# Operand work of the up units moved later in the MLP of a two-layer decoder trunk, and split in two parts

## The chip, the cores and the metric

The kernel runs on one core of one Trainium2 chip. The metric is device time in microseconds (us) of one execution; lower is better. The kernel before takes 2268.28 us, the median of 3 runs (2266.05 to 2270.3).

The engines of the core work side by side, each through its own queue in order: TensorE (PE; its weight loads are listed as PEld), VectorE (DVE), ScalarE (ACT), GpSimd (POOL), and SyncE (SP), which issues the DMA transfers. Matrix products add up in PSUM, which has eight banks of 128 x 512 f32.

## The reference

Two layers work on x of 256 tokens by 2048 features, all in float32. The attention part of each layer (a gated linear attention and a stick-breaking attention side by side, and an output projection added to x) is untouched by the change but for its last addition. What matters here is the second half of a layer:

```python
hm = rms_norm(x, mlp_norm)
up = jnp.square(jax.nn.relu(jnp.einsum('bsd,df->bsf', hm, w_up)))     # 2048 -> 8192
return x + jnp.einsum('bsf,fd->bsd', up, w_down)                       # 8192 -> 2048
```

## The kernel before

**Products.** Each f32 matrix is split into a high part (rounded by an ACT copy to the matmul's fp32r form) and a low part (a DVE subtraction: the value less its high part). A product of two blocks is three matmuls: high x high, high x low weights, low x high weights (`mm`, lines 989 to 998). So for each block of weights that the DMA brings (tile `raw`), ACT makes `whi` (L985) and DVE makes `wlo` (L986), with four tiles of each.

**Units and steps.** The MLP of a layer is 16 units: for each quarter q of the 8192 hidden features up 0, up 1, down 0, down 1. A unit is 8 steps, j = 0 to 7; each multiplies a 256 x 256 piece of the operand by 256 x 1024 weights. Steps 1, 3 and 5 are "fast": they use seven block products in place of eight, for which DVE first forms sums of weight blocks (`ts` at L1118, then two additions through `add`, L1001), and which need further sums of the operand's blocks (`sx`). A fast step is four products with 6, 3, 6 and 6 matmuls, any other step is two with 12 each, so a unit is 22 products, k = 0 to 21, and 183 matmuls. Step j=1 is k = 2 to 5, j=3 is k = 8 to 11, j=5 is k = 14 to 17.

**Order.** In the MLP the order of PE, DVE and ACT is written out by hand. The main loop (L1188 to 1207) prepares the weights of product k+3 (ACT and DVE rows) and then emits product k on PE (`emit`, L1173), so weights are prepared four products ahead. After emitting product k it runs what hangs on k: the tail of the unit (k = 17: sums of four banks; 20 and 21: the other four) and the entries of the table that `begin` returns (L1149). So a row that hangs on k stands in the queues of ACT and DVE behind the preparation of product k+3 and ahead of that of k+4.

**Operands.** The result of an up unit has to become the operand of the down units. In the unit that follows (the second up unit, or the first down unit), `begin` gives: at k = 0 and 1 `turn`: PE transposes the result into banks 5, 7 and 1, 6, eight transposes each, and ACT squares them into `t` (L1086); at k = 3, 4, 9, 10 `operand`, which calls `forms` for the four pieces. `forms` makes high and low part of a piece through `split` (L294: an ACT copy, L295, and a DVE subtraction, L296). For a fast piece (number 1, 3 or 5 of the eight) it first does four DVE subtractions (L305 to 308) into `e`, splits `e` into `sx` and then the piece itself. The second up unit makes pieces 0 to 3, of which 1 and 3 are fast; the first down unit makes 4 to 7, of which 5 is fast, and uses them itself, from j=4 (k = 12) on.

**Start of the MLP.** The output projection adds into `acc` tiles of two banks; `residual` (L940) adds the result to x. For the last of the four blocks of columns, `residual(3, uo)` stands in the MLP's loop, behind the preparation of product 2. The MLP's banks take the place of the projection's `acc` and `ps` tiles in PSUM, in the order in which they are first asked for: 2, 4, 5, 7, 3, 8, 1, 6, so banks 2 and 4 of the first product lie on the last projection's `acc`. The last block of x is turned and becomes an operand after product 0 (`norm_operand`, L339 on DVE, banks 5 and 7).

## Time and profile before

| | |
|---|---|
| median of 3 runs | 2268.28 us (2266.05 to 2270.3) |
| profiled execution | 2270.26 us, of which the span from the first to the last instruction is 2268.6 |
| busy, share of the span | PE 2213.3 us (98%), DVE 1825.4 (80%), ACT 1250.8 (55%), POOL 38.0 (2%) |
| mean granted TensorE clock | 0.989 |
| DMA | 408.96 MB, mean 180 GB/s |
| MLP of the first layer | 419.88 us to some 1135 us of the span; of the second from 1546.27 us to the end |

In the profile, "busy" is the time in which an engine's instructions run. A row of a timeline gives start and duration in us, engine, source line, operation, the tile written and the tiles read, and in brackets the idle time before it and what ended that. "x3" means that three like rows in a row are merged. In a window's row each engine has its busy time and, in brackets, its instructions; then come the granted clock, the DMA's share and GB/s. The granted clock is a share of TensorE's full rate.

### The profile page before, as it was taken

To read this page: it belongs to the slowest core of one execution; us is meant where nothing else is said; L and a number is where in the kernel's file an instruction comes from. 1 tells how busy PE (TensorE), PEld (TensorE's weight loads), DVE (VectorE), ACT (ScalarE), POOL (GpSimd) and SP (SyncE) were. 2 spreads that over 40 slices of the span, in tenths; PEclk is the share of its full clock that TensorE was granted. 3 is DMA by queue.
4 is the path that set the end of the run, shared out by engine and by line. 5 is a ranking of instruction groups with operands and counts; after the bars stand their busy time and mean duration, and the time that the engine had idled before them with its cause. 6 is when DMAs were issued, how large, how long until landed. Compare 5 with 4: busy or idle time off the path is not lost.

```text
span 2268.6 us, 27081 instructions
## 1 busy us (share of the span) xinstructions
PE 2213.3 (98%) x10376; PEld 1822.8 (80%) x10376; DVE 1825.4 (80%) x2286; ACT 1250.8 (55%) x1623; POOL 38.0 (2%) x64
## 2 busy tenths in 40 slices
PE   9999999999999999999999999999999999999999
PEld 7988778777877877877888887887778778778777
DVE  5777566789988989988966765667899889889888
ACT  5555355555565556455556553555655555654664
POOL 0020000000000000000000200000000000000000
PEclk9999999999999999999999999999999999999999
DMA  6554446454545555555446543555455545455544
GB/s 226 186 165 153 149 148 240 165 190 164 215 171 174 213 184 177 202 186 185 152 157 195 171 162 133 185 204 188 165 186 199 185 173 202 171 186 212 187 158 146
DMA packets 152549, 408.96 MB, mean 180 GB/s; under 512 B 6650, under 2 KB 31810, under 8 KB 152420
## 3 DMA queue, kind: packets, MB, share of 16 engines
q1 hardware_dynamic: 152420, 407.24, 51.8%
q8 instruction: 81, 1.33, 0.2%
q14 instruction: 48, 0.39, 0.1%
HBM read 405.12 MB, written 2.10 MB: 180 GB/s over the span
## 4 chain that ended last, share of the span: by engine, by line
PE 85%; DVE 11%; ACT 3%; issue 1%; DMA 0%; SPq 0%; POOL 0%; ACTq 0%
PE acc L412 9%; PE acc L413 9%; PE acc L414 9%; DVE wlo L986 4%; PE acc L459 3%; PE acc L463 1%; DVE act L296 1%; DVE ts L1118 1%; ACT whi L985 1%; DVE raw L1001 1%; DVE t L1001 1%; ACT act L1086 1%; DVE sx L296 1%; ACT sx L295 1%; PE ps L882 1%
## 5 line engine op out<-in xcount | busy, mean ns | idle before, releaser
L986 DVE TENSOR_TENSOR wlo<-raw,whi 128x1024 fp32r<-128x1024 f32 x512 | 610.1, 1221 | 82.4 <-ACT whi L985 79.3
L985 ACT ACTIVATE whi<-raw 128x1024 fp32r<-128x1024 f32 x512 | 532.8, 1056 | 198.4 <-PE acc L414 10.0
L395 DVE TENSOR_TENSOR wlo<-raw,whi 128x1024 fp32r<-128x1024 f32 (+2 forms) x274 | 317.5, 1165 | 194.9 <-ACT whi L393 193.7
L393 ACT ACTIVATE whi<-raw 128x1024 fp32r<-128x1024 f32 (+2 forms) x274 | 273.5, 1004 | 290.9 <-PE acc L414 243.1
L412 PE MATMUL acc<-whi,act 128*128 128x512 f32 (+2 forms) x960 | 368.7, 384 | 1.6 <-ACT act L337 1.6
L413 PE MATMUL acc<-wlo,act 128*128 128x512 f32 (+2 forms) x960 | 362.4, 378 | 0.0
L414 PE MATMUL acc<-whi,act 128*128 128x512 f32 (+2 forms) x960 | 362.0, 377 | 0.0
L985 ACT ACTIVATE whi<-t 128x512 fp32r<-128x512 f32 x96 | 60.7, 632 | 280.6 <-DVE t L1001 189.1
L412 PEld LDWEIGHTS acc<-whi,act 128*128 128x128 f32 x960 | 181.1, 189 | 36.8 <-issue 4.1
L414 PEld LDWEIGHTS acc<-whi,act 128*128 128x128 f32 x960 | 180.8, 188 | 34.0 <-issue 0.7
L413 PEld LDWEIGHTS acc<-wlo,act 128*128 128x128 f32 x960 | 181.1, 189 | 31.7 <-DVE wlo L395 0.8
L986 DVE TENSOR_TENSOR wlo<-ts,whi 128x1024 fp32r<-128x1024 f32 x96 | 117.6, 1225 | 16.3 <-ACT whi L985 16.3
L1118 DVE TENSOR_TENSOR ts<-raw 128x1024 f32<-128x1024 f32 x96 | 117.0, 1219 | 0.0
L985 ACT ACTIVATE whi<-ts 128x1024 fp32r<-128x1024 f32 x96 | 100.5, 1047 | 0.0
L459 PE MATMUL acc<-act,whi 128*128 128x512 f32 x256 | 91.9, 402 | 0.0
L463 PE MATMUL acc<-act,wlo 128*128 128x256 f32 x256 | 71.8, 280 | 0.0
L1047 ACT ACTIVATE act<-act,st 128x512 f32<-128x512 f32 x64 | 44.6, 720 | 48.7 <-DVE act L1001 48.7
L1001 DVE TENSOR_TENSOR raw<-ts,raw 128x512 f32<-128x512 f32 x96 | 66.4, 692 | 3.3
L1001 DVE TENSOR_TENSOR t<-raw 128x512 f32<-128x512 f32 x96 | 66.4, 692 | 3.3
L986 DVE TENSOR_TENSOR wlo<-t,whi 128x512 fp32r<-128x512 f32 x96 | 65.7, 684 | 0.0
L459 PEld LDWEIGHTS acc<-act,whi 128*128 128x128 f32 x256 | 48.1, 188 | 11.1
L295 ACT ACTIVATE sx<-t 128x384 fp32r<-128x384 f32 x24 | 12.6, 526 | 69.6 <-DVE t L308 69.6
(2384 smaller groups left out, 4670.7 us busy)
## 6 DMA issues: line engine op xcount, KB each, us to landing
raw<-in_w_up_dram SPq DMA_DIRECT2D x128, 1024.0 KB, 5.1
raw<-in_w_down_dram SPq DMA_DIRECT2D x128, 1024.0 KB, 5.4
raw<-in_w_in_dram SPq DMA_DIRECT2D x84, 1024.0 KB, 5.1
raw<-in_w_o_dram SPq DMA_DIRECT2D x32, 1024.0 KB, 5.0
raw<-in_w_in_dram SPq DMA_DIRECT2D x14, 512.0 KB, 6.7
raw<-in_w_in_dram SPq DMA_DIRECT2D x8, 544.0 KB, 3.7
out_dram<-xb SPq DMA_DIRECT2D x8, 256.0 KB, 2.0
xb<-in_x_dram SPq DMA_DIRECT2D x3, 512.0 KB, 8.0
```

The source lines that it names most:

```text
L296: nc.vector.tensor_tensor(d[:, :, 1, :], t, f32(d[:, :, 0, :]), ALU.subtract)
L393: newest["hi"] = nc.scalar.activation(h, r, AF.Copy).ins
L395: newest["lo"] = nc.vector.tensor_tensor(lo[:, q : q + step, :width], r, f32(h), ALU.subtract).ins
L412: nc.tensor.matmul(o, xh[:, sl], whi[:, j, :width], start=first, stop=False)
L413: nc.tensor.matmul(o, xh[:, sl], wlo[:, j, :width], start=False, stop=False)
L414: st["mm"] = nc.tensor.matmul(o, xl[:, sl], whi[:, j, :width], start=False, stop=last).ins
L459: nc.tensor.matmul(acc[:, f, :], whi[:, j, sl], op.both(k), start=(k == 0), stop=False, skip_group_check=True,)
L463: nc.tensor.matmul(acc[:, f, T:], wlo[:, j, sl], xh, start=False, stop=(k == KT - 1), skip_group_check=True,)
L985: nc.scalar.activation(hi[:, :n], r, AF.Copy)
L986: nc.vector.tensor_tensor(lo[:, :n], r, f32(hi[:, :n]), ALU.subtract)
L1001: nc.vector.tensor_tensor(dst, a, b, ALU.subtract if sub else ALU.add)
L1118: nc.vector.tensor_tensor(t13, ends, b12.unsqueeze(1).to_broadcast([P, 2, 512]), ALU.add)
```

## The change

Four edits, all in the MLP:

1. `split` does its ACT copy at once and returns the DVE subtraction as a function; `forms` returns a function that does the subtractions of its pieces. `begin` runs that function one product later than `forms`.
2. The squares leave `turn` and become `square`, one product later: at k = 1 and 2.
3. The pieces are made at k = 4, 10, 13 and 15 (before 3, 4, 9, 10), their low parts at 5, 11, 14 and 16.
4. The MLP's banks are asked for at once, in the order 5, 7, 1, 6, 2, 4, 3, 8; and `residual(3, uo)` stands behind the preparation of product 1, no longer of product 2.

```diff
+    def new_bank(m):
+        return pools["m"].tile([P, 512], F32, tag=f"m{m}", name=nm(f"m{m}_"))
+    unused = {}
     def mlp_psum():
         open_scope("psum", m=1)
+        unused.update((m, new_bank(m)) for m in (5, 7, 1, 6, 2, 4, 3, 8))
     def bank(m):
-        return pools["m"].tile([P, 512], F32, tag=f"m{m}", name=nm(f"m{m}_"))
+        return unused.pop(m, None) or new_bank(m)
...
     def split(d, t):
         nc.scalar.activation(d[:, :, 0, :], t, AF.Copy)
-        nc.vector.tensor_tensor(d[:, :, 1, :], t, f32(d[:, :, 0, :]), ALU.subtract)
+        return lambda: nc.vector.tensor_tensor(
+            d[:, :, 1, :], t, f32(d[:, :, 0, :]), ALU.subtract
+        )
     def forms(op, i, t, tag):
+        lows = []
...
-            split(d, e)
-        split(op.pair(i), t)
+            lows.append(split(d, e))
+        lows.append(split(op.pair(i), t))
+        return lambda: [low() for low in lows]
...
-                nc.scalar.activation(t[:, i].rearrange("p j t -> p (j t)"), pt, AF.Square)
+        def square(u, h):
+            y = ys[u]
+            t = y["t", h] = act_tile(F32, (P, 2, 2, T))
+            for i in range(2):
+                nc.scalar.activation(
+                    t[:, i].rearrange("p j t -> p (j t)"), y["p", h, i], AF.Square
+                )
         def operand(u, i):
...
-            forms(op, 4 * n2 + i, ys[u]["t", i // 2][:, i % 2], "sx")
+            ys[u]["low", i] = forms(op, 4 * n2 + i, ys[u]["t", i // 2][:, i % 2], "sx")
...
-            return {
-                0: lambda: turn(p, 0), 1: lambda: turn(p, 1),
-                3: lambda: operand(p, 0), 4: lambda: operand(p, 1),
-                9: lambda: operand(p, 2), 10: lambda: operand(p, 3),
+            work = {
+                0: lambda: turn(p, 0),
+                1: lambda: (turn(p, 1), square(p, 0)),
+                2: lambda: square(p, 1),
             }
+            for i, k in enumerate((4, 10, 13, 15)):
+                work[k] = lambda i=i: operand(p, i)
+                work[k + 1] = lambda i=i: ys[p]["low", i]()
+            return work
...
-                    if x == 1 and i == 0:
+                    if x == 0 and i == 1:
                         residual(3, uo)
```

What moves, at three places. In the rows, `wlo` and `whi` are the low and high parts of weights, `raw` the weights as loaded, `ts` and `t` the sums of a fast step (and `t` also the sums `e` of a fast piece), `act` the pieces and their sources, `sx` the rounded sums of a fast piece. The lines of the changed kernel are numbered 8 to 19 higher (L986 is L999 there, L296 is L304, L1118 is L1137, L1001 is L1014, L985 is L998, L295 is L303).

The first place is DVE in the first layer's unit 1 (a second up unit), from the low part of product 7 to that of product 8. Before:

```order
L986 TENSOR_TENSOR wlo_4076<-raw_728_3871,whi_4075 128x1024
L305 TENSOR_TENSOR t_775_4087<-act_4009 128x128
L306 TENSOR_TENSOR act_4009<-act_4009 128x128
L307 TENSOR_TENSOR t_775_4087<-act_4009 128x128
L308 TENSOR_TENSOR t_775_4087<-act_4009,t_775_4087 128x128
L296 TENSOR_TENSOR sx_4088<-t_775_4087,sx_4088 128x3x128
L296 TENSOR_TENSOR act_4095<-act_4009,act_4095 128x2x256
L1118 TENSOR_TENSOR ts_4100<-raw_733_3890 128x1024
L1001 TENSOR_TENSOR raw_733_3890<-ts_4100,raw_733_3890 128x512
L1001 TENSOR_TENSOR t_780_4101<-raw_733_3890 128x512
L986 TENSOR_TENSOR wlo_4106<-raw_733_3890,whi_4105 128x1024
```

Now:

```order
L999 TENSOR_TENSOR wlo_4073<-raw_728_3871,whi_4072 128x1024
L1137 TENSOR_TENSOR ts_4088<-raw_733_3890 128x1024
L1014 TENSOR_TENSOR raw_733_3890<-ts_4088,raw_733_3890 128x512
L1014 TENSOR_TENSOR t_777_4089<-raw_733_3890 128x512
L999 TENSOR_TENSOR wlo_4094<-raw_733_3890,whi_4093 128x1024
L304 TENSOR_TENSOR act_4084<-act_4047,act_4084 128x2x256
L999 TENSOR_TENSOR wlo_4107<-t_777_4089,whi_4106 128x512
```

The four subtractions and two low parts of fast piece 1 have left this place; the low part of piece 0, which stood ahead of product 7's part, follows product 8's. Piece 1's subtractions now stand at the same place one fast step later, ahead of the `ts` of product 14, and its two low parts behind product 14's.

The second place is ACT in the same unit, from the high part of product 17 on. Before (L1055 copies a bank for the unit's tail):

```order
L985 ACTIVATE whi_4241<-raw_3964 128x1024
L985 ACTIVATE whi_4253<-raw_4063 128x1024
L985 ACTIVATE whi_4260<-raw_4063 128x1024
L985 ACTIVATE whi_4272<-raw_778_4098 128x1024
L1055 ACTIVATE act_4282<-m__783_4109 128x512
```

Now:

```order
L998 ACTIVATE whi_4229<-raw_3964 128x1024
L998 ACTIVATE whi_4242<-raw_4063 128x1024
L303 ACTIVATE sx_4250<-t_811_4249 128x3x128
L303 ACTIVATE act_4256<-act_4060 128x2x256
L998 ACTIVATE whi_4258<-raw_4063 128x1024
L998 ACTIVATE whi_4272<-raw_775_4086 128x1024
L1068 ACTIVATE act_4282<-m__780_4097 128x512
```

The two high parts of fast piece 3 now stand ahead of product 19's. On DVE, at the same place of the changed kernel:

```order
L304 TENSOR_TENSOR act_4227<-act_4060,act_4227 128x2x256
L999 TENSOR_TENSOR wlo_4243<-raw_4063,whi_4242 128x1024
L317 TENSOR_TENSOR t_811_4249<-act_4060 128x128
L318 TENSOR_TENSOR act_4060<-act_4060 128x128
L319 TENSOR_TENSOR t_811_4249<-act_4060 128x128
L320 TENSOR_TENSOR t_811_4249<-act_4060,t_811_4249 128x128
L999 TENSOR_TENSOR wlo_4259<-raw_4063,whi_4258 128x1024
L304 TENSOR_TENSOR sx_4250<-t_811_4249,sx_4250 128x3x128
L304 TENSOR_TENSOR act_4256<-act_4060,act_4256 128x2x256
L999 TENSOR_TENSOR wlo_4273<-raw_775_4086,whi_4272 128x1024
```

Piece 3's subtractions follow product 18's low part, and product 19's low part follows them with no sums of a fast step between. In a first down unit the piece made here (7) isn't fast, and only its one low part stands behind product 19's.

The third place is DVE at the start of the first layer's MLP, from product 1's low part to that of product 3. Before (`xb_104` is the last block of x):

```order
L986 TENSOR_TENSOR wlo_3613<-raw_656_3598,whi_3612 128x1024
L1118 TENSOR_TENSOR ts_3618<-raw_657_3600 128x1024
L1001 TENSOR_TENSOR raw_657_3600<-ts_3618,raw_657_3600 128x512
L1001 TENSOR_TENSOR t_667_3619<-raw_657_3600 128x512
L986 TENSOR_TENSOR wlo_3624<-raw_657_3600,whi_3623 128x1024
L940 TENSOR_TENSOR xb_104<-acc_3420,xb_104 128x1024
L986 TENSOR_TENSOR wlo_3629<-t_667_3619,whi_3628 128x512
```

Now:

```order
L999 TENSOR_TENSOR wlo_3621<-raw_664_3606,whi_3620 128x1024
L953 TENSOR_TENSOR xb_104<-acc_3420,xb_104 128x1024
L1137 TENSOR_TENSOR ts_3627<-raw_665_3608 128x1024
L1014 TENSOR_TENSOR raw_665_3608<-ts_3627,raw_665_3608 128x512
L1014 TENSOR_TENSOR t_675_3628<-raw_665_3608 128x512
L999 TENSOR_TENSOR wlo_3633<-raw_665_3608,whi_3632 128x1024
L999 TENSOR_TENSOR wlo_3637<-t_675_3628,whi_3636 128x512
```

The last addition to x has moved ahead of the sums of step 1. The first product's banks, 2 and 4, now lie on the projection's `ps` tiles, and banks 5, 7, 1 and 6 on its two `acc` tiles. On PE, SP and POOL the order of instructions is the same in both kernels.

More of the change, by code (lines that the diff above doesn't have):

```diff
@@ L329, in norm_operand @@
                     )
-                forms(op, 2 * n + h2, t, "sxh")
+                forms(op, 2 * n + h2, t, "sxh")()
                 continue
@@ L1075, in turn @@
             y = ys[u]
-            t = y["t", h] = act_tile(F32, (P, 2, 2, T))
             for i in range(2):
-                pt = bank(((5, 7), (1, 6))[h][i])
+                pt = y["p", h, i] = bank(((5, 7), (1, 6))[h][i])
                 for j in range(2):
```

## The prediction

> **What bounds the kernel now.** I read the page first, then the unit lengths in windows, then what TensorE (PE) waits for, then the granted clock around one wait, then the chain of waits that leads into it.

> ```profile
> PE 2213.3 (98%) x10376; PEld 1822.8 (80%) x10376; DVE 1825.4 (80%) x2286; ACT 1250.8 (55%) x1623; POOL 38.0 (2%) x64
> ```

> PE is busy 98% of the span of 2268.6 us, so only its gaps and its clock can give time. Units are the 16 blocks of 8 steps of a layer's MLP, numbered 0 to 15 in the order up 0, up 1, down 0, down 1. Windows over five units (columns: length, then busy time of PE, weight loads, VectorE (DVE), ScalarE (ACT), GpSimd, then clock):

> ```profile
> 462.70:511.00 48.30, 45.48 (x200) 36.97 (x200) 42.41 (x53) 28.94 (x38) 0.00 (x0) 0.96 0.50 173
> 511.00:558.30 47.30, 45.21 (x200) 37.10 (x200) 42.28 (x51) 27.87 (x35) 0.00 (x0) 0.96 0.46 159
> 558.30:599.80 41.50, 41.50 (x184) 34.34 (x184) 39.05 (x44) 21.75 (x23) 0.00 (x0) 1.00 0.57 204
> 599.80:641.30 41.50, 41.50 (x184) 34.38 (x184) 37.67 (x41) 22.40 (x25) 0.00 (x0) 1.00 0.62 224
> 869.70:915.40 45.70, 43.63 (x201) 35.77 (x199) 41.92 (x51) 27.67 (x35) 0.00 (x0) 1.00 0.47 164
> ```

> Units 3 and 4 (rows three and four) have no operand work and run at PE's pace: 183 matmuls in 41.5 us, 0.227 us each. Units 1, 2 and 10 (the first two rows and the last) turn the up unit before them and make its operands; they take 45.7 to 48.3 us, and 16 of the 32 units are of this kind. Their 16 transposes cost some 2 us (unit 10: 45.7, less 41.5, less one gap of 2.2), so such a unit at PE's pace would take 43.5 us. DVE is busy 42.4 us in unit 1: it has about 1 us to spare in those 43.5.

> What PE waits for (the source line of the second matmul of a product, whose weights are the low part that DVE makes):

> ```profile
>   DVE wlo L986: 43.0, 24
> ```

> 24 gaps hold 43.0 us of idle; counted from matmul start to matmul start, less the normal 0.23, about 47 us. One of them in PE's timeline:

> ```profile
> 710.82 0.50 PE L997 MATMUL m__1134_5775<-wlo,act 128*128 128x512 f32 x1 [2.07 <-DVE wlo L986]
> ```

> Windows of PE alone (length, busy, clock), and the mean clock:

> ```profile
> 708.50:711.90 3.40, 1.33 (x7) 1.00 0.00 1
> 711.90:715.30 3.40, 3.40 (x10) 0.51 0.15 22
> 886.00:889.40 3.40, 1.51 (x7) 1.00 0.34 137
> 889.40:892.80 3.40, 3.21 (x14) 1.00 0.00 0
> ```
> ```profile
> core 0: 2268.6 us, clock 0.989
> ```

> They show a second price: after the gap of 2.07 us, which leaves PE busy 1.33 of 3.4 us, the next 3.4 us run at clock 0.51; where the busy part was 1.51 (a gap across two windows) the clock stays 1.00. The mean clock of 0.989 is 0.011 x 2268.6 = 25 us lost, some 14 such windows at 1.7 us. Gaps and slow clock together: about 71 us. The chain of waits into the gap at 673.8 us (unit 5):

> ```profile
> 655.39 0.30 DVE t L308
> 655.71 0.54 ACT sx L295
> 656.27 0.56 DVE sx L296
> 656.83 0.65 DVE act L296
> 657.49 1.15 DVE ts L1118
> ...
> 660.08 2.71 DVE wlo L986 x3
> ```

> The four subtractions of a fast operand end, ACT rounds the result, DVE waits and makes two low parts, and only then starts on the sums of the next fast step. All of it stands between two low parts that PE needs.

> **The change, part by part.** No row moves on PE, SP or POOL, and no step that moves issues a DMA; what moves is on DVE and ACT. Product k below is the k-th of a unit's 22; each low part is queued some four products ahead. How far ahead, in a unit without operand work, the clean unit 4 shows:

> ```profile
> 620.43 1.22 DVE L1118 TENSOR_TENSOR ts<-raw 128x1024 f32<-128x1024 f32 x1
> ...
> 623.02 1.22 DVE L986 TENSOR_TENSOR wlo<-raw,whi 128x1024 fp32r<-128x1024 f32 x1
> 624.15 0.69 DVE L986 TENSOR_TENSOR wlo<-t,whi 128x512 fp32r<-128x512 f32 x1
> 624.84 1.23 DVE L986 TENSOR_TENSOR wlo<-ts,whi 128x1024 fp32r<-128x1024 f32 x1
> 627.05 4.80 DVE L986 TENSOR_TENSOR wlo<-raw,whi 128x1024 fp32r<-128x1024 f32 x4 [0.99 <-ACT whi L985]
> ...
> 634.42 2.35 DVE L986 TENSOR_TENSOR wlo<-raw,whi 128x1024 fp32r<-128x1024 f32 x2
> ```

> On PE, the matmul of that unit's product 14 that reads the low part; and on DVE, unit 3's low part of product 21 (the first of the three):

> ```profile
> 625.93 0.39 PE L997 MATMUL m__982_5069<-wlo,act 128*128 128x512 f32 x1
> ```
> ```profile
> 595.45 3.49 DVE L986 TENSOR_TENSOR wlo<-raw,whi 128x1024 fp32r<-128x1024 f32 x3
> ```

> Product 14's low part ends at 624.24 and PE needs it at 625.93: spare 1.7 us. Counting 0.227 us per matmul onward, the spare is 2.4 at product 15, 1.85 at 16, 1.0 at 17, 1.15 at 18, 2.7 at 19, 4.3 at 20 and 3.2 at 21 (row 634.42); in the down unit before it 21 has only 0.7 (row 595.45), since eight additions precede it. DVE idles once, 0.99 us before product 17's part.

> *Gap at product 8 (step j=3).* Gone from ahead of it: four subtractions, ACT's turn, two low parts and operand 0's, some 3.7 us. Operand 0's low part now follows product 8's, and 0.6 us fits the spare of the later ones. The squares leave ACT's queue for one and two prepared parts later; the banks they free are first needed at products 4 and 5, and PE takes 2.7 us for each of products 0 and 1, which covers them. I take this gap, and its half clock, as gone: spare about 1.5 us.

> *Product 14 to 18 (j=5, j=6).* Inserted now: subtractions 1.3 (four at 0.33 pitch) ahead of 14, low parts of 0.5 and 0.6 ahead of 15. Spare 1.7 - 1.3 = 0.4 at 14; 2.4 - 2.4 = 0 at 15; 1.85 - 2.4 = -0.6 at 16. A stall of about 0.7 with the 0.1 that lies between a part's end and its matmul when PE waits. In the down unit the same operand is used at once: its low part ends 1.1 us after product 14's, so PE waits 0.6 there, inside the same 0.7. The idle 0.99 before 17 absorbs part; operand 2's low part adds 0.6: 2.4 - 1.0 + 0.6 = 2.05 against 1.15 at 18. Lost so far: 0.95.

> *Product 19 in a second up unit.* Operand 3 is fast there: four subtractions on DVE, and in ACT's queue its two high parts now stand ahead of product 19's high part, with nothing on DVE between. The same sequence in unit 1 of before, on DVE and on ACT:

> ```profile
> 476.77 0.29 DVE L308 TENSOR_TENSOR t<-act,t 128x128 f32<-128x128 f32 x1
> ```
> ```profile
> 477.09 0.53 ACT L295 ACTIVATE sx<-t 128x384 fp32r<-128x384 f32 x1 [2.94 <-DVE t L308]
> 477.52 0.62 ACT L295 ACTIVATE act<-act 128x512 fp32r<-128x512 f32 x1
> 478.05 1.04 ACT L985 ACTIVATE whi<-raw 128x1024 fp32r<-128x1024 f32 x1
> ```

> From the last subtraction's start to the end of the following high part: 2.3 us, where DVE would need 0.33 to go on. Before, the sums of a fast step lay behind it and filled DVE's time; now DVE waits 2.05. Charge at 19: 2.05 + 1.3 + 2.05 = 5.4 against 2.7. Lost so far 2.8, of which the new gap is some 1.5 us of idle in two pieces. At 20 and 21 two more low parts (1.1): 6.5 against 3.2. Lost in the whole unit: about 3.4 us.

> *Product 21 in a first down unit.* Operand 7 isn't fast, so no turn of ACT; its low part adds 0.6: 2.05 + 0.6 = 2.65 against 0.7. Lost: 2.1 us, and the next unit, which starts with DVE 0.6 later than before, loses about 0.2.

> *Start of the MLP.* PE's wait for the last residual block goes, but not what hangs on it:

> ```profile
> 419.88 0.47 PE L995 MATMUL m__672_3632<-whi,act 128*128 128x512 f32 x1 [1.92 <-DVE xb L940]
> ```
> ```profile
> 418.52 1.22 DVE L940 TENSOR_TENSOR xb<-acc,xb 128x1024 f32<-128x1024 f32 x1
> ...
> 423.86 0.49 DVE L339 SCALAR_TENSOR_TENSOR act<-m__674_3646,gcol_b,act 128x256 fp32r<-128x256 f32 x1 [3.52 <-ACT act L337]
> ...
> 427.25 1.23 DVE L986 TENSOR_TENSOR wlo<-ts,whi 128x1024 fp32r<-128x1024 f32 x1 [0.47 <-ACT whi L985]
> ```

> The accumulator is complete at about 418.0, and the addition now starts near 418.1. The sums of step 1 (2.6 us) and two low parts (1.8) used to run largely before that and now follow: 418.1 + 1.15 + 2.6 + 1.8 = 423.65 for the first L339, 0.2 earlier than 423.86. From there to product 4's low part nothing changes (3.4 us). PE starts 2.1 us earlier and waits about 1.9 more at product 4. I count 0.2 per layer, 0.4 in all; the ends are 0 and the whole 4.2.

> **The sum.** 8 x (3.4 + 2.1 + 0.2) = 45.6 us come back of the 71; with 0.4 from the start the gain is 26 us. No half-clock window is left in it: the largest new gap leaves PE busy about 1.9 of 3.4 us, above the 1.51 that kept the clock. The profiled execution took 2270.26 us (1.7 outside the span), 2 above the median of 2268.28; I take the gain off the median: 2242 us.

> [...]

> **The rivals.**
> - *ACT's turn is covered.* If product 19's high part waited for nothing, units lose 1.35 (1.95 fewer, at 19 to 21), 2.1 and 0.2: 29 us return, 2226 us. For it: ACT is busy only 29 of 48 us. Against: its queue is in order, and rows 477.09 to 478.05 show the high part starting right behind.
> - *The half clock comes at the new gap.* If 1.5 us of idle are enough, 8 windows at 1.7 us: 2256 us. Against: the row with 1.51 busy, idle 1.9, at full clock after.
> - *Slower.* The same mechanism, grown: the gap at product 19 and the one at product 21 of the down unit each last 0.8 us longer, PE falls under 1.45 busy in a 3.4 us window, and both cost a half window. Per group 5.7 + 2 x (0.8 + 1.7) = 10.7, in all 86 against 71: 2283 us. For it: DVE has 1 us to spare per unit. It decides where a gap leaves PE less than 1.45 busy.
> [...]

> **How the numbers follow.** Forecast 0.62, covered turn 0.15, half clock 0.12, slower 0.05, windows stay 0.03, elsewhere 0.03. The range 2225 to 2257 reaches to the second and third case. A measurement of this kernel tells about 0.2% (4.5 us) from no change; faster by more: 0.62 + 0.15 + 0.12 + 0.01 = 0.90, within 0.05, slower 0.05.

> **What would show it.** Right: no PE wait at product 8; second up units near 46.9 us, first down units near 45.6, clock 1.00 in them; a PE wait on the low part at product 19, behind ACT's high part, behind the fast operand's rounding; the first product of the MLP at once, and a wait at its fifth. Wrong: units 1 and 2 at 43.5 (DVE had more room than counted), or clock 0.5 windows still there.

## The result and the profile after

The changed kernel takes 2238.25 us, the median of 4 runs (2237.89 to 2238.47), beside 2268.76 us for the kernel before (4 runs, 2266.05 to 2270.3). The ratio is 0.9867, with a 95% interval of 0.985 to 0.9884: 30.5 us less. The profiled executions differ by 32.4 us: 2237.89 against 2270.26, and spans of 2236.2 against 2268.6; that of before lies 1.5 us above the median, that of the changed kernel 0.4 below. The line numbers of the new kernel are those given with the change (`whi` L998, `wlo` L999, the three matmuls of a product L1008, L1010, L1011, additions L1014).

The page's first part, and the clock:

```profile
PE 2201.8 (98%) x10376; PEld 1800.9 (81%) x10376; DVE 1818.7 (81%) x2286; ACT 1246.2 (56%) x1623; POOL 38.0 (2%) x64
```
```profile
core 0: 2236.2 us, clock 1.000
```

PE's share looks as before, and says little: a matmul at half clock counts as busy (PE is busy 3.41 of 3.41 us at clock 0.50 in a row of the squares alone, below). The clock says more. It was 0.989 and is 1.000, so no window at half clock is left in the MLP. The windows over the same five units (1, 2, 3, 4 and 10; length, then PE, weight loads, DVE, ACT, GpSimd, clock):

```profile
462.10:508.60 46.50, 44.79 (x200) 35.48 (x199) 40.94 (x52) 27.17 (x36) 0.00 (x0) 1.00 0.46 158
508.60:554.00 45.40, 44.25 (x200) 35.76 (x200) 42.86 (x53) 29.18 (x37) 0.00 (x0) 1.00 0.53 187
554.00:595.60 41.60, 41.60 (x184) 34.42 (x185) 39.17 (x44) 21.67 (x23) 0.00 (x0) 1.00 0.57 206
595.60:637.00 41.40, 41.40 (x184) 34.31 (x183) 37.58 (x41) 22.37 (x25) 0.00 (x0) 1.00 0.61 224
858.60:903.90 45.30, 44.17 (x199) 35.65 (x200) 42.75 (x53) 29.11 (x37) 0.00 (x0) 1.00 0.53 186
```

Unit 1 went from 48.3 to 46.5 us and unit 2 from 47.3 to 45.4. Counted from first matmul to first matmul, the eight second up units took 390.4 us together and now take 372.1, the eight first down units 376.7 and now 362.8: 32.2 us less in 16 units. Before, their lengths varied (48.2 to 49.6, depending on where the half clock fell); now all second up units lie between 46.50 and 46.53. Units 3 and 4 are as they were. The spans differ by 32.4, so the gain lies in the units whose operand work moved.

What PE waits for, by the releaser of the second matmul of a product (low part of the weights), and of the first:

```profile
  DVE wlo L999: 15.2, 26
```
```profile
  ACT whi L998: 4.3, 10
  DVE act L1014: 1.4, 8
  DVE xb L1014: 0.9, 5
```

The low parts cost 15.2 us of idle instead of 43.0. No wait is left at product 8. DVE there (unit 1) runs from the sums of the fast step straight to product 8's low part, and piece 0's follows it:

```profile
474.29 1.22 DVE L1137 TENSOR_TENSOR ts<-raw 128x1024 f32<-128x1024 f32 x1
...
476.88 1.22 DVE L999 TENSOR_TENSOR wlo<-raw,whi 128x1024 fp32r<-128x1024 f32 x1
478.01 0.68 DVE L304 TENSOR_TENSOR act<-act,act 128x512 fp32r<-128x512 f32 x1
```

The new waits stand at the end of the unit. PE in unit 1: product 19 twice, product 21, and the next unit's first product:

```profile
498.42 0.50 PE L1008 MATMUL m__759_4023<-whi,act 128*128 128x512 f32 x1 [0.42 <-ACT whi L998]
499.68 0.50 PE L1010 MATMUL m__759_4023<-wlo,act 128*128 128x512 f32 x1 [0.76 <-DVE wlo L999]
...
505.66 0.50 PE L1010 MATMUL m__759_4023<-wlo,act 128*128 128x512 f32 x1 [0.25 <-DVE wlo L999]
...
508.63 0.47 PE L1008 MATMUL m__836_4375<-whi,act 128*128 128x512 f32 x1 [0.18 <-DVE act L1014]
```

DVE and then ACT at the same place:

```profile
496.05 0.29 DVE L320 TENSOR_TENSOR t<-act,t 128x128 f32<-128x128 f32 x1
498.40 1.22 DVE L999 TENSOR_TENSOR wlo<-raw,whi 128x1024 fp32r<-128x1024 f32 x1 [2.06 <-ACT whi L998]
```
```profile
496.38 0.53 ACT L303 ACTIVATE sx<-t 128x384 fp32r<-128x384 f32 x1 [3.92 <-DVE t L320]
496.81 0.62 ACT L303 ACTIVATE act<-act 128x512 fp32r<-128x512 f32 x1
497.33 1.99 ACT L998 ACTIVATE whi<-raw 128x1024 fp32r<-128x1024 f32 x2
```

This is the chain of the prediction: the fourth subtraction ends, ACT (idle 3.92 us until then) rounds both parts of the piece, only then product 19's weights, and DVE idles 2.06 us.

The start of the MLP, on PE (first product and product 4) and on DVE:

```profile
417.54 0.39 PE L1008 MATMUL m__659_3599<-whi,act 128*128 128x512 f32 x1
...
426.61 0.50 PE L1008 MATMUL m__691_3709<-whi,act 128*128 128x512 f32 x1 [0.52 <-ACT whi L998]
427.87 0.50 PE L1010 MATMUL m__691_3709<-wlo,act 128*128 128x512 f32 x1 [0.76 <-DVE wlo L999]
```
```profile
417.74 1.23 DVE L953 TENSOR_TENSOR xb<-acc,xb 128x1024 f32<-128x1024 f32 x1 [3.12 <-PE acc L427]
418.88 1.22 DVE L1137 TENSOR_TENSOR ts<-raw 128x1024 f32<-128x1024 f32 x1
```

PE starts 2.3 us earlier and gives most of it back at product 4: unit 0 ends at 462.12 instead of 462.74. Of these 0.6 us, 0.26 lie ahead of the MLP: the projection's last matmul ends at 417.70 in this profile and at 417.96 in that of before. DVE idles 3.12 us for the accumulator with the sums of step 1 queued behind the addition.

### The profile page after: what moved, and what is told of

The parts are those of the page before. It is cut to its first block, busy times and chain, and to the rows that moved or that the text cites. A ratio compares the mean times of both kernels' runs of the same rounds, so it can differ in the third digit from the quotient of the medians.

```text
span 2236.2 us, 27047 instructions
## 1 busy us (share of the span) xinstructions
PE 2201.8 (98%) x10376; PEld 1800.9 (81%) x10376; DVE 1818.7 (81%) x2286; ACT 1246.2 (56%) x1623; POOL 38.0 (2%) x64
## 3 DMA queue, kind: packets, MB, share of 16 engines
q8 instruction: 81, 1.33, 0.2%
## 4 chain that ended last, share of the span: by engine, by line
PE 81%; DVE 15%; issue 2%; ACT 1%; DMA 0%; SPq 0%; POOL 0%; DVEq 0%; ACTq 0%
PE acc L425 9%; PE acc L426 9%; PE acc L427 9%; DVE wlo L999 7%; PE acc L472 3%; PE acc L476 1%; DVE xb L1014 1%; ACT whi L998 1%; DVE t L1014 1%; DVE act L304 1%; DVE ts L1137 1%; DVE act L1014 1%; DVE sx L304 1%; PE ps L895 1%; PE ps L907 1%
## 5 line engine op out<-in xcount | busy, mean ns | idle before, releaser
L999 DVE TENSOR_TENSOR wlo<-raw,whi 128x1024 fp32r<-128x1024 f32 x512 | 610.4, 1220 | 96.4 <-ACT whi L998 92.9
L998 ACT ACTIVATE whi<-raw 128x1024 fp32r<-128x1024 f32 x512 | 528.8, 1054 | 185.2 <-PE acc L427 10.0
L998 ACT ACTIVATE whi<-t 128x512 fp32r<-128x512 f32 x96 | 60.8, 633 | 268.7 <-DVE t L1014 143.0
L999 DVE TENSOR_TENSOR wlo<-ts,whi 128x1024 fp32r<-128x1024 f32 x96 | 117.4, 1223 | 1.4 <-ACT whi L998 1.4
L1137 DVE TENSOR_TENSOR ts<-raw 128x1024 f32<-128x1024 f32 x96 | 116.7, 1216 | 0.0
L998 ACT ACTIVATE whi<-ts 128x1024 fp32r<-128x1024 f32 x96 | 100.4, 1046 | 0.0
L1014 DVE TENSOR_TENSOR raw<-ts,raw 128x512 f32<-128x512 f32 x96 | 66.4, 692 | 3.3
L1014 DVE TENSOR_TENSOR t<-raw 128x512 f32<-128x512 f32 x96 | 66.4, 692 | 3.3
L999 DVE TENSOR_TENSOR wlo<-t,whi 128x512 fp32r<-128x512 f32 x96 | 65.7, 684 | 0.0
L303 ACT ACTIVATE sx<-t 128x384 fp32r<-128x384 f32 x24 | 12.6, 526 | 73.9 <-DVE t L320 73.9
```

The lines of the kernel that those rows point to most:

```text
L998: nc.scalar.activation(hi[:, :n], r, AF.Copy)
L999: nc.vector.tensor_tensor(lo[:, :n], r, f32(hi[:, :n]), ALU.subtract)
L1014: nc.vector.tensor_tensor(dst, a, b, ALU.subtract if sub else ALU.add)
L1137: nc.vector.tensor_tensor(t13, ends, b12.unsqueeze(1).to_broadcast([P, 2, 512]), ALU.add)
```

## The experiments

The theory was the prediction's: the chain subtractions, rounding, low parts ahead of a product's low part is what stopped PE; splitting it takes the wait away, moving it puts its remains at product 19; and the half clock follows the long gaps. Twelve kernels tested its steps. Beside them the kernel before had medians of 2266.5 to 2268.5 us; each ratio is against the runs of the same chip.

### Each edit alone, on the kernel before

**Edit 4 alone** (banks and last residual block):

```diff
-        return pools["m"].tile([P, 512], F32, tag=f"m{m}", name=nm(f"m{m}_"))
+        return unused.pop(m, None) or new_bank(m)
...
-                    if x == 1 and i == 0:
+                    if x == 0 and i == 1:
                         residual(3, uo)
```

> Kernel before with the fourth edit alone (order of the banks, last residual block behind product 1). Theory (the wait is only moved: the addition now stands ahead of the sums of step 1, so product 4 waits instead): the 1.92 us wait at each layer's first product is gone, a wait of about 1.3 us in two pieces stands at product 4, and the time falls by 0.5 to 1 us, to about 2268. Rival (the wait at the start is a loss of its own): 4.2 us less, 2264.5, and no wait at product 4.

Measured: 2266.85 us, ratio 0.9989 (0.9976 to 1.0002), no difference that can be told; the rival's 4.2 us lie in this interval too, so the time does not decide. The waits do: the one of 1.92 us at the first product is gone, and product 4 waits 0.51 and 0.77 us in its place. The theory holds.

**Edit 2 alone** (squares one product later):

```diff
-                0: lambda: turn(p, 0), 1: lambda: turn(p, 1),
+                0: lambda: turn(p, 0),
+                1: lambda: (turn(p, 1), square(p, 0)),
+                2: lambda: square(p, 1),
```

> Kernel before with the second edit alone (squares one product later). Theory (the gaps come from what stands between two low parts on VectorE; the squares only let product 6's low part start 0.3 us earlier): the gap at product 8 shrinks from 2.07 to about 1.8 us and stays, so that fewer half-clock windows follow it, while the gap at product 14 in second up units grows to 2 us where no slow window came before it; about 2260. Rival (ScalarE's early squares hold up the weights and make the gap): the gap at product 8 goes, below 2245.

Measured: 2261.77 us, 0.9976 (0.9965 to 0.9987), about 6.7 us less. The size came as expected, one step of the reasoning did not: the half clock hardly became rarer (the granted clock of the runs is 0.990 in the mean, that of the kernel before 0.989). The gap at product 8 in unit 1 shrank from 2.08 to 1.79 us; here it is, and the clock's windows around it:

```profile
482.10 0.50 PE L997 MATMUL m__753_3995<-wlo,act 128*128 128x512 f32 x1 [1.79 <-DVE wlo L986]
```
```profile
480.00:483.41 3.41, 1.62 (x8) 1.10 (x7) 3.38 (x5) 2.39 (x3) 0.00 (x0) 1.00 0.00 0
483.41:486.82 3.41, 3.41 (x10) 2.64 (x9) 3.41 (x5) 2.67 (x4) 0.00 (x0) 0.50 0.27 36
```

PE was busy 1.62 of 3.41 us, and the next window still ran at half clock. So the early squares cost a few tenths of a microsecond each time, and only the split or the move takes the clock's price away.

**Edit 1 alone** (the split in two parts, at the old places 3, 4, 9 and 10):

```diff
-        nc.vector.tensor_tensor(d[:, :, 1, :], t, f32(d[:, :, 0, :]), ALU.subtract)
+        return lambda: nc.vector.tensor_tensor(
+            d[:, :, 1, :], t, f32(d[:, :, 0, :]), ALU.subtract
+        )
...
+            for i, k in enumerate((3, 4, 9, 10)):
+                work.setdefault(k + 1, []).append(lambda i=i: ys[p]["low", i]())
+                work.setdefault(k, []).append(lambda i=i: operand(p, i))
```

> Kernel before with the first edit alone: low parts one product later, pieces still made at 3, 4, 9 and 10. Theory (order of the queues alone; ScalarE's turn lies beside the sums of a fast step here, at product 19 of the changed kernel it lies beside nothing): the gap at product 8 falls to 0.4 us, small waits follow at 9, 10 and 14 to 16, none at 19; a second up unit loses 2.9 us, a first down unit 1.2; no half-clock window; about 2231, so less than the whole change. Rival (the gain comes from making the pieces later): gaps of 1 to 2 us stay at products 8 and 14, 2250 or more.

Measured: 2235.3 us, 0.9857 (0.9837 to 0.9877). This one edit gives 33 us, more than all four together: no run of it took over 2236.31 us and none of the changed kernel under 2237.89, and its second up units take 46.3 us and its first down units 44.95, against 46.5 and 45.35. Its waits in unit 1, products 8, 10, 14 and 16:

```profile
482.06 0.50 PE L1001 MATMUL m__753_3995<-wlo,act 128*128 128x512 f32 x1 [0.41 <-DVE wlo L990]
484.87 0.50 PE L1001 MATMUL m__773_4078<-wlo,act 128*128 128x512 f32 x1 [0.16 <-DVE wlo L990]
493.79 0.50 PE L1001 MATMUL m__753_3995<-wlo,act 128*128 128x512 f32 x1 [0.46 <-DVE wlo L990]
496.60 0.50 PE L1001 MATMUL m__773_4078<-wlo,act 128*128 128x512 f32 x1 [0.17 <-DVE wlo L990]
```

Four small waits (1.2 us) in place of two long ones (2.8 us in this unit before, and half clock behind the first), and none at product 19, since no fast piece is made there. The first product of each layer still waits 1.92 us, and in the first layer half clock seems to follow that wait: matmuls into the bank `m__673`, from 421.1 us on, take up to 0.63 us, like those in the half-clock window of the squares alone, and not 0.39.

**Edit 3 alone** (the new places, piece in one part):

```diff
-                3: lambda: operand(p, 0), 4: lambda: operand(p, 1),
-                9: lambda: operand(p, 2), 10: lambda: operand(p, 3),
+                4: lambda: operand(p, 0), 10: lambda: operand(p, 1),
+                13: lambda: operand(p, 2), 15: lambda: operand(p, 3),
```

> Kernel before with the third edit alone: pieces at 4, 10, 13 and 15, high and low parts together. Theory: the gap at product 8 is gone; 3.0 us stand ahead of product 14's low part against 1.7 spare, a wait of about 1.4 us there; at product 19 of a second up unit the turn of ScalarE is uncovered, as in the changed kernel; 3.4 us lost in a second up unit, 2.6 in a first down unit; no half-clock window; about 2247. Rival (the later places are the whole gain, the split adds nothing): 2238.

Measured: 2246.26 us, 0.9904 (0.9884 to 0.9925). In unit 1 of this kernel:

```profile
492.32 0.50 PE L997 MATMUL m__753_3995<-wlo,act 128*128 128x512 f32 x1 [1.19 <-DVE wlo L986]
500.22 0.50 PE L995 MATMUL m__760_4026<-whi,act 128*128 128x512 f32 x1 [0.18 <-ACT whi L985]
501.48 0.50 PE L997 MATMUL m__760_4026<-wlo,act 128*128 128x512 f32 x1 [0.76 <-DVE wlo L986]
```

The move alone breaks up the long gap too (1.19 us at product 14), and it alone already makes the waits at product 19. In the order shown (4, 2, 1, 3) the edits alone give 1.6, 6.7, 33.2 and 22.2 us, 63.7 in all, and together 30.5: the split and the move are two cures for one gap.

### What the rest hangs on, changed in the changed kernel

**The new places taken back**, all else kept:

```diff
-            for i, k in enumerate((4, 10, 13, 15)):
+            for i, k in enumerate((3, 4, 9, 10)):
```

> The changed kernel with the pieces back in their old places 3, 4, 9 and 10; what stays of the change is the split in two parts a step apart, the later squares, the banks and the residual block. It prices the new places alone. Theory (the split is what gained; the new places put the last piece's four subtractions and ScalarE's turn where VectorE has nothing else to do, and cost more than they bring): 2228 us, the split alone having given 2235.3 with the old squares and banks. Rival (the new places are needed, since products 8 and 14 get too little spare without them): 2238 or more.

Measured: 2231.55 us, 0.9843 (0.9829 to 0.9856). Between the two numbers, on the theory's side: the new places cost 6.7 us once the split is there. Second up units take 46.2 us, first down units 44.86.

**The last piece's high parts behind product 19's.** `forms` here returns a function for the high parts, which returns one for the low parts; for each piece the table holds three products (subtractions, high parts, low parts):

```diff
-            for i, k in enumerate((4, 10, 13, 15)):
+            plan = ((4, 4, 5), (10, 10, 11), (13, 13, 14), (15, 16, 17))
```

> The changed kernel with one move: the two high parts of the last piece (sub-step 15, fast in second up units) stand on ScalarE behind product 19's high part, not ahead of it; their low parts follow one step later. Theory (VectorE's wait of 2.06 us for ScalarE, behind the four subtractions, is what stops TensorE at product 19): the two waits at product 19 (0.42 and 0.76) shrink to under 0.2, second up units go from 46.5 to about 44.9, first down units stay at 45.35: 8 x 1.6 = 13 less, 2225 us. Rival (VectorE is full there and the wait only moves to product 21 or the next unit): second up units stay over 46, 2234 or more.

Measured: 2228.58 us, 0.9836 (0.9817 to 0.9854); second up units 45.4, first down units 45.36 as before. 1.1 us of the expected 1.6 came. On DVE, product 19's low part now follows at once, and the wait is at product 20's, 0.93 us:

```profile
495.47 0.29 DVE L320 TENSOR_TENSOR t<-act,t 128x128 f32<-128x128 f32 x1
495.68 1.22 DVE L1003 TENSOR_TENSOR wlo<-raw,whi 128x1024 fp32r<-128x1024 f32 x1
497.83 1.23 DVE L1003 TENSOR_TENSOR wlo<-raw,whi 128x1024 fp32r<-128x1024 f32 x1 [0.93 <-ACT whi L1002]
```

PE no longer waits at product 19, but 0.86 us at 21. So ACT's turn did stop PE there, and about a third of the charge moved on, as the rival has it.

**The four subtractions on GpSimd:**

```diff
+            eng = nc.gpsimd if tag == "sx" else nc.vector
...
-            nc.vector.tensor_tensor(e[:, 2, :], a21, a11, ALU.subtract)
+            eng.tensor_tensor(e[:, 2, :], a21, a11, ALU.subtract)
```

(and so for the other three).

> The changed kernel with the four subtractions of each fast piece on GpSimd instead of VectorE (both fast pieces of a second up unit, at the same places). Theory (VectorE's load, 2.6 us of subtractions per second up unit, and its wait behind them are the whole loss): VectorE goes straight from product 18's low part to 19's, second up units near 43.9, first down units stay unless they have a fast piece: 8 x 2.6 = 21 less, 2217 us, at best 2207 with the down units' piece relieved too. Rival (GpSimd takes several times as long per subtraction, so the rounding on ScalarE, and product 19's high part queued behind it, wait longer than now): over 2240 us, a longer wait at product 19 on ScalarE's high part.

Measured: 2202.54 us, 0.972 (0.9704 to 0.9736), better than the theory's best. Units 1 and 2:

```profile
463.10:506.30 43.20, 43.20 (x200) 35.96 (x199) 40.31 (x45) 28.09 (x37) 6.26 (x8) 1.00 0.53 178
506.30:550.50 44.20, 43.78 (x200) 35.77 (x199) 41.05 (x48) 28.50 (x36) 2.81 (x4) 1.00 0.54 183
```

The second up unit now runs at PE's pace, 43.3 us from first matmul to first matmul, so all 3.2 us that it lost go with the subtractions and the wait behind them. I had sized the theory at 2.6 us per unit, the subtractions alone. The piece's rounding on ACT no longer waits for DVE's queue, so product 19's high part comes early as well. The rival expected GpSimd to be slow; it is (0.46 to 1.34 us a subtraction in unit 1, against 0.29 in the row of DVE at 496.05 us of the changed kernel), but not where it matters: its queue is not part of the written order, and it makes the sums long before they are rounded (last section). So this kernel changes the engine of the subtractions and their time; the next one leaves them on DVE and changes their place alone.

**Each piece in three parts, at the products with most spare time**, nothing taken off DVE (first down units have 13, 13 and 15 for the last piece):

```diff
+            plan = ((4, 4, 5), (2, 4, 9), (8, 8, 12), (15, 16, 21))
```

> The changed kernel with subtractions, high parts and low parts in three separate steps, each at the product with the most spare time as read from the profile of after: the subtractions stay in places 4, 4 or 2, 8 and 15 (13 in down units), high parts at 4, 4, 8, 16 (13), low parts at 5, 9, 12 and 21 (15). Theory (the loss that is left, 3.0 us in second up units and 1.9 in first down units, is short spare at single products, not VectorE's total): second up units 43.5 to 44, first down units about 44, 8 x (2.6 + 1.3) = 31 less, 2207 us. Rival (VectorE is full over the whole unit, 2.06 us idle in unit 2 and 5.06 in unit 1, so that the loss only moves): 2225 or more, with new waits at products 8 to 12 or at the next unit's start.

Measured: 2206.98 us, 0.9739 (0.9724 to 0.9755): the theory's number, by two errors that cancel, which is luck. Second up units take 43.3 us, 3.2 less where 2.6 was expected, and first down units 44.66, 0.7 less where 1.3 was. DVE does the same work as in the changed kernel (1815.8 us in all, there 1818.7), 39.85 us of it in unit 1, and no product of that unit waits:

```profile
462.00:505.30 43.30, 43.30 (x201) 35.78 (x199) 39.85 (x50) 27.10 (x36) 0.00 (x0) 1.00 0.51 172
```

So DVE was not full over a second up unit; it was full from product 14 on. In first down units, with DVE busy 43.5 of 44.6 us, the rival is half right.

**The residual block's addition back behind the sums of step 1:**

```diff
-                    if x == 0 and i == 1:
+                    if x == 1 and i == 0:
                         residual(3, uo)
```

> The changed kernel with the last residual block's addition back behind the sums of step 1, as before; the new order of the banks is kept. Theory (the banks' order takes the wait at the first product away, the addition's early place only pushes the sums of step 1, and with them the chain to product 4, 1.2 us back): TensorE still starts at once, the wait at product 4 (0.52 and 0.76) gets shorter by about 1.2, two layers: 2 to 3 less, 2236 us. Rival (the early addition is needed, since the bank that it reads is taken by an early product): the wait at a product of the first unit on the addition comes back, 2238 or more.

Measured: 2234.46 us, 0.9861 (0.9845 to 0.9877), 3.8 us less than the changed kernel. DVE at the start, and product 4 on PE:

```profile
414.84 1.22 DVE L1137 TENSOR_TENSOR ts<-raw 128x1024 f32<-128x1024 f32 x1
...
418.57 1.22 DVE L953 TENSOR_TENSOR xb<-acc,xb 128x1024 f32<-128x1024 f32 x1
```
```profile
426.24 0.39 PE L1008 MATMUL m__691_3709<-whi,act 128*128 128x512 f32 x1
426.46 0.43 PE L1010 MATMUL m__691_3709<-wlo,act 128*128 128x512 f32 x1
```

The sums run while DVE used to idle, both waits at product 4 are gone, and unit 0 takes 42.74 us instead of 44.59. The order of the banks is the half of edit 4 that helps; the early addition gives the gain away.

### Together, and the other way

**GpSimd's subtractions and the residual block together:**

```diff
+            eng = nc.gpsimd if tag == "sx" else nc.vector
...
-                    if x == 0 and i == 1:
+                    if x == 1 and i == 0:
```

> The changed kernel with two single changes together: the subtractions of the fast pieces on GpSimd, and the last residual block's addition back behind the sums of step 1. Theory (the two losses lie in different units and add): 2238.3 less 35.7 less 3.8, 2198.8 us; second up units 43.3, first down units 44.2, the MLP's first unit 42.75. Rival (they overlap, because the first unit's lateness is handed on to the second): 2201 to 2203.

Measured: 2199.03 us (2198.89 to 2199.52), 0.9699 (0.9686 to 0.9712). The two add up, and this is the fastest kernel of the study: 39 us below the changed one, 68 below the one before.

**The same, with the pieces of first down units in their old places:**

```diff
-            for i, k in enumerate((4, 10, 13, 15)):
+            for i, k in enumerate((3, 4, 9, 12) if units[u][1] else (4, 10, 13, 15)):
```

> The same two changes, and in first down units the pieces stand in the old places 3, 4, 9 and 12 instead of 4, 10, 13 and 15 (second up units keep the new ones). Theory (what first down units still lose, 44.2 against 43.5, is VectorE's work after product 13, while it idles 2.7 us before product 7; work put into that idle time is free): first down units 43.5 to 43.7, 8 x 0.55 = 4.4 less, 2194.5 us. Rival (the pieces' low parts push product 7's and 8's own past their spare of about 1 us, so the loss only changes its place): 2198 or more, with waits at products 7 to 10 of units 2, 6, 10 and 14.

Measured: 2200.43 us, 0.9704 (0.9691 to 0.9718). The rival's side: first down units take 44.28 us instead of 44.17. In unit 2 PE lost, from matmul start to matmul start, 0.6 us at product 21 and 0.3 at the next unit's first product; now it loses 0.2 at product 10, 0.25 at 17, 0.15 at 21 and the same 0.3. So the loss changed its place. DVE's idle time early in unit 2 is still there:

```profile
512.36 1.23 DVE L1000 TENSOR_TENSOR wlo<-raw,whi 128x1024 fp32r<-128x1024 f32 x1 [1.28 <-ACT whi L999]
514.55 1.23 DVE L1000 TENSOR_TENSOR wlo<-raw,whi 128x1024 fp32r<-128x1024 f32 x1 [0.96 <-ACT whi L999]
```

It lies ahead of the pieces' places and waits for ACT's high parts; the pieces went behind it. Of the 0.9 us that these units still lose, the 0.3 at the next unit's first product are a wait for the tail's additions, in both kernels; what would take it away is not tested.

**More subtractions**, to see the price and the clock. The first subtraction of each fast piece is done four times, with the same values:

```diff
+            for _ in range(4 if tag == "sx" else 1):
-            nc.vector.tensor_tensor(e[:, 2, :], a21, a11, ALU.subtract)
+                nc.vector.tensor_tensor(e[:, 2, :], a21, a11, ALU.subtract)
```

> The changed kernel with the first of the four subtractions of each fast piece of the MLP's up units done four times over (the same values written again), so 3 more subtractions at 0.33 us, 1.0 us of VectorE per fast piece, two pieces in a second up unit and one in a first down unit. Theory (VectorE has no room from product 14 on, and a gap that leaves TensorE idle about 2 us in one 3.4-us window slows its clock in the next): about 0.6 to 1.0 is lost for each piece, 8 x (0.6 + 1.0 + 0.9) = 20 more, and the two waits at product 19 grow together to some 2.2 us of idle, so half clock follows in second up units, up to 8 x 1.7 = 13.6 more: 2265 to 2272 us, clock under 0.997. Rival 1 (the clock does not follow such gaps): 2256 to 2260, clock 1.000. Rival 2 (VectorE has room after all): under 2245.

Measured: 2262.86 us, 0.998 (0.9971 to 0.999), clock 0.998. Second up units take 48.46 to 48.50 us in six cases, 2.0 more than the changed kernel for 2.0 us of added subtractions; first down units 46.32, 1.0 more for 1.0. So from product 14 on, a microsecond of DVE is a microsecond of PE. In units 1 and 5 the second up unit took 49.2 us. There the two waits at product 19 (1.39 and 0.76 us) fell into one window of the clock, in unit 5 as a whole and in unit 1 but for 0.4 us of the first, and the next window ran at half rate. Unit 1:

```profile
499.48:502.89 3.41, 1.70 (x6) 1.19 (x7) 2.48 (x4) 3.41 (x5) 0.00 (x0) 1.00 0.13 14
502.89:506.30 3.41, 3.41 (x10) 2.62 (x9) 3.34 (x5) 1.28 (x2) 0.00 (x0) 0.50 0.84 298
```

The clock does follow such gaps, so rival 1 falls. It followed in two units of eight and not in all, and cost 0.7 us there instead of 1.7, since DVE catches up while PE is slow: the waits that unit 9 still has at product 21 and at the next unit's first product are missing in unit 1. Hence the time is a little below the theory's range.

## Why the prediction was right, and where its terms were off

The forecast was 2242 us and the result is 2238.25; the likeliest case came, by its mechanism, and so did all its signs: no wait at product 8, second up units of 46.5 us (46.9 written) and first down units of 45.35 (45.6), full clock, the wait at product 19 behind ACT's turn, and the one at the MLP's fifth product. The closeness of the number is in part luck: in the spans the gain is 6.4 us larger than the 26 forecast, but the profiled execution of before, from which the terms were read, lay 2 us above the median off which they were taken. Point by point:

- **Gap at product 8 and its half clock gone.** So it was; the spare there is 1.7 us, predicted 1.5. Edit 3 alone takes the gap away and edit 1 alone leaves 0.41 us of it; with either no half clock follows it (clock 1.00 over units 1 and 2 of both).
- **Product 14 to 18.** Predicted loss 0.95 in unit 1. Measured from start to start: 0.44 us at product 16 and 0.15 at 18, some 0.6. This term was over-sized. Product 15, whose spare of 2.4 the prediction counted as used up, still had 0.20 us (its low part is done at 491.15, its matmul starts at 491.35), so what was put in ahead of it takes some 2.25 us and not 2.4; the rest of the difference is not settled. In unit 2 PE loses 0.5 us at product 14, for the low part of the piece that it uses at once (predicted 0.6).
- **Product 19.** The uncovered turn of ACT was put at 2.05 us and DVE idles 2.06. It sets the two waits there (0.42 and 0.76 of idle, 1.75 us from start to start; the prediction charges 1.85). That it is the turn and not DVE's load alone, the kernel with the high parts behind product 19's shows: 1.1 us less per unit.
- **The whole unit.** Predicted losses against PE's pace of 43.5 us: 3.4 and 2.1, and 0.2 handed on. Measured on the same scale 3.0, 1.85 and 0.1. The pace itself is 43.3, as the kernel with GpSimd shows (the transposes cost 1.8 us, not 2), which makes the pool of before 74 us instead of 71.
- **Handed to the next unit.** It is not DVE's later start on weights, as the prediction had it, but a wait of 0.18 us for the tail's additions, which read the banks of the next unit's first product. From start to start it costs 0.3 us ahead of that product, which the lengths above hold already, and 0.1 in the next unit. This wait was not foreseen.
- **Start.** Predicted 0.2 per layer, measured 0.4: from the end of the projection's last matmul to the first of unit 1 it takes 44.42 us instead of 44.78, and 44.38 instead of 44.76 in the second layer. The mechanism is the one that was written: the addition pushes the sums. That it need not, the prediction did not ask; moved back, the start gives 1.8 more per layer.
- **The sum.** Predicted return 8 x (3.4 + 2.1 + 0.2) = 45.6, measured 8 x (3.0 + 1.85 + 0.1) = 39.6: 6.0 us of the mis-sized terms, and 0.3 more from the start. 26 + 6.0 + 0.3 = 32.3, against 32.4 between the spans. The medians differ by 30.5, since the profiled execution of before lay 1.5 us above the median of its four runs and that of the changed kernel 0.4 below its own.
- **The clock.** Right in the result (1.000), too generous in the argument. That the clock holds above 1.51 us busy was read from one window; with squares alone a window with 1.62 busy was followed by half clock, and with more subtractions one with 1.70. Around the two waits at product 19 of the changed kernel, PE is busy so long:

```profile
496.50:499.90 3.40, 2.23 (x9) 1.33 (x8) 1.50 (x2) 3.40 (x6) 0.00 (x0) 1.00 0.40 160
```

  2.23 us (the prediction expected 1.9), and the clock holds there. The margin to 1.70 is half a microsecond, less than the row of 1.51 promised.
- **The rivals.** "ACT's turn is covered" fell with the 2.06 us of idle. "The half clock comes at the new gap" did not happen, but 2 us more of subtractions in each second up unit brought it in two units of eight. "Slower" needed still more than that: with 1 us more per fast piece the kernel is still 0.2% faster than the one before. Its 1.45 us busy was an estimate between the 1.33 that half clock followed and the 1.51 that it did not; half clock came after 1.62 and 1.70 us too. The case that the slow windows stay (0.03) did not come: the clock is 1.000.

What the prediction did not weigh is that the edits could work against each other. It took the four as one and asked what the sum would be; the split alone is 3 us faster than all four, and the early addition of edit 4 takes back what its order of the banks gives.

## What to carry to other kernels

When an engine's queue is written in order, read the spare time product by product, not its busy share: DVE at 81% had no room after product 14 and idled 2 us before product 7, and a chain put where nothing else fills the queue leaves it idle during the turns of other engines (2.06 us of DVE here, 1.1 us of PE). Split such a chain before moving it, and put each part where the rows show spare time, or give the small operations to an idle engine: that was worth 31 to 36 us here, as much as the whole change. And price the edits one by one; two cures for the same gap do not add.

## What the runs showed of the hardware

**GpSimd beside DVE.** In the kernel with the subtractions on GpSimd, a subtraction of 128x128 takes 0.46 us while DVE idles and 1.3 us while DVE makes a low part; DVE is slowed too. GpSimd and DVE in unit 1:

```profile
472.79 0.47 POOL L319 TENSOR_TENSOR act<-act 128x128 f32<-128x128 f32 x1
473.33 1.32 POOL L320 TENSOR_TENSOR t<-act 128x128 f32<-128x128 f32 x1
474.73 1.33 POOL L321 TENSOR_TENSOR t<-act,t 128x128 f32<-128x128 f32 x1
```
```profile
472.95 2.79 DVE L1000 TENSOR_TENSOR wlo<-raw,whi 128x1024 fp32r<-128x1024 f32 x2 [0.98 <-ACT whi L999]
475.66 1.48 DVE L1138 TENSOR_TENSOR ts<-raw 128x1024 f32<-128x1024 f32 x1
```

Two low parts take 2.36 us elsewhere, and `ts` 1.22, so DVE lost 0.7 us here, against 2.6 for the subtractions of two pieces of its own. The subtraction at 472.79, which starts while DVE idles, keeps its 0.47 us, and those at 473.33 and 474.73, which start while DVE makes the two low parts, take 1.32 and 1.33; what holds them is not shown. GpSimd stands outside the written order and makes both pieces as soon as their squares are there, some 17 us ahead of the second one's rounding at 493.2 us, so its 3.0 and 3.8 us per piece cost PE nothing.
